# A hybrid decoder layer's list schedule: small VectorE instructions and the shared SBUF port, and a choice that is left open while the port is taken

## The chip, the cores and the metric

The kernel runs on one core of a Trainium2 chip. The metric is the device time of one execution in microseconds, as the median of several runs. Five engines work beside each other: TensorE (PE) for matmuls, with its weight loads shown apart (PEld), VectorE (DVE), ScalarE (ACT), GpSimd (POOL), and SyncE (SP), which issues the DMAs. "Busy" is the time in which an engine executes; "idle before" is the gap ahead of an instruction and the instruction or transfer that ended it.

## The reference, cut to what matters

One decoder layer, batch 1, 512 tokens, 1024 channels, all float32. Two attention branches run over the same normalized input, are merged by gates and followed by an MLP with 4096 hidden channels:

```python
h = rmsnorm(x, ln_mix_g[l])
proj = h @ w_in[l]
(dq, dk, dv, nq, kc, vc, ksl, vsl, kwn, vwn, ng, mg) = jnp.split(proj, split_at, axis=-1)
dq = rope(rmsnorm(dq.reshape(B, S, DIFF_HEADS, 2, HEAD_DIM), diff_q_norm_g[l]), pos)
...
y_diff = diff_attention(dq, dk, dv, lam, lambda_init, diff_subln_g[l])
...
y_nsa = nsa_attention(nq, k_cmp, v_cmp, k_slc, vsl.reshape(B, S, G, HEAD_DIM), k_win,
                      vwn.reshape(B, S, G, HEAD_DIM), nsa_gates)
merge = jax.nn.sigmoid(mg).reshape(B, S, 2, D)
mixed = merge[:, :, 0] * (y_diff @ w_proj_diff[l]) + merge[:, :, 1] * (y_nsa @ w_proj_nsa[l])
x = x + mixed @ w_out[l]
h = rmsnorm(x, ln_mlp_g[l])
x = x + jnp.square(jax.nn.relu(h @ w_mlp_up[l])) @ w_mlp_down[l]
```

The first branch is a differential attention of 8 heads (two softmaxes, one subtracted from the other with a factor lam); the second has 16 heads in 4 groups with a compressed, a selected and a windowed part.

## The kernel before, in words

**Precision.** Every float32 matmul is made of three with rounded operands. An operand is split into a high part (a cast) and a low part (what is left: operand minus high part), and the products high by high, low by high and high by low are summed. For weights the DMA brings `wraw` (128 x 1024), `whi` is its cast and `wlo` the subtraction, each done in two halves of 512 columns; both have two buffers, and so has `wraw`. The same splitting makes `qa` and `qb` from transposed queries, `kp` from transposed keys (one buffer; DMAs carry it on to `kk`), `ah` and `al` from transposed probabilities, `vt`, `big`, `kk` and others.

**Stages.** Up to some 665 us the kernel projects the input piece by piece (matmuls into `gb`), normalizes and rotates queries and keys (`str` are their inverse norms, made by POOL with a power, `t1r` and `t2r` the products of the rotation, `rw` the result), transposes them (`ptp`), and runs the score, softmax and value steps of both branches (`sb`, `p`, `sm`, `pta`, `av` for the first; `sbc`, `sc`, `st`, `smn`, `ptn`, `avn` for the second). A small side work makes the compressed keys (`hb`, `o`, `st2`, `ct1`, `ct2`). From some 665 us the branches' outputs are multiplied with their projections (`big`, `tm`, `kk`), then with w_out, and from some 700 us the MLP runs: matmuls of 512 columns without a break, for which weights are split.

**What sets the order.** The program does not issue instructions as it meets them. Each is recorded by `note` with a priority (the order of recording, with 15 places' advance for hot streams), what it depends on, the engines that may do it (`ways`) with a planned duration for each (`price`), and whether it uses the SBUF port that DVE and POOL share (`ported`). `flush` then plans the whole program, and issues all instructions in the order of planned starts, so that every engine's order is fixed before the kernel runs; line 357 is the one line that issues, and all rows of the trace carry it. The planner takes the engine that can go on first, and of its ready instructions the one with the best priority. `self.port` is the time until which the shared port is planned to be taken.

Some instructions may go to either of two engines: the cast `whi` to ACT or DVE, the subtraction `wlo` to DVE or POOL, the products `t1r` and `t2r` and their sum to DVE or POOL, some additions of `tm` to DVE or POOL, copies and other casts to ACT or DVE. Whichever engine the planner serves first, with that instruction on top, gets it.

Before the change, `ported` said no for any instruction whose largest operand has fewer than 64 elements a partition. An instruction that uses the port, met while the port was taken, was passed over if the engine had a ready one that doesn't use it; if it had none, the one with the best priority was tied to this engine, with its start put off until the port comes free.

Of the kernel before, what the change touches and what calls it, by code (L numbers as in the profile page):

```python
# [14 lines left out]
OP = mybir.AluOpType  # L15
# [116 lines left out]
class Sched:  # L132
# [34 lines left out]
    def price(self, eng, method, aps, k):  # L167
        if "accum_out" in k:
            aps = [x for x in aps if x is not k["accum_out"]]
        n = max(self.size(x) for x in aps)  # L170
        psum = any(self.tiles[x.tensor.name].space == "PSUM" for x in aps if x.tensor.name in self.tiles)
        if eng == "PE":
            if method == "transpose":
                return 113.0
            return max(113.0, 5.5 + self.size(aps[-1]) * 0.4315)
        if eng == "ACT":
            return (51 if psum else 93) + n * 0.8333 + (93 if "accum_out" in k else 0) + (
                93 if any(self.size(x) == 1 for x in aps[1:]) and n > 1 else 0)
        if eng == "DVE":
            ptr = sum(1 for x in aps[1:] if self.size(x) == 1) if n > 1 else 0  # L180
            if method in ("tensor_scalar", "tensor_copy") and not psum:
                return 69 + n * 0.52 + 61 * ptr
            if method == "memset":
                return 8 + n * 1.04
            if method == "reciprocal":
                return 69 + n * 6.25
            return 69 + n * 1.042 + 61 * ptr
        if eng == "POOL":
            if k.get("op") == OP.pow:
                return 300 + n * 165.0  # L190
            return 150 + n * 2.1
        return 20.0
# [2 lines left out]

    def ported(self, eng, method, aps, k):

        if max(self.size(x) for x in aps) < 64:
            return False
        if eng == "POOL":  # L200
            return k.get("op") != OP.pow
        return eng == "DVE" and method in self.TWICE and not any(
            self.tiles[x.tensor.name].space == "PSUM" for x in aps if x.tensor.name in self.tiles)

# [67 lines left out]
    def flush(self):  # L272
# [34 lines left out]
        while len(done) < len(ops):  # L307
            best = None
            for e in self.free:
                for h, k in ((self.wait[e], 2), (ok[e], 1)):  # L310
                    while h and h[0][k].left == -1:
                        heapq.heappop(h)
                t = self.free[e] if ok[e] else max(self.free[e], self.wait[e][0][0]) if self.wait[e] else None
                if t is not None and (best is None or t < best[0]):
                    best = (t, e)
            assert best is not None, "no instruction can go on"
            t, e = best
            while self.wait[e] and self.wait[e][0][0] <= t:
                _, p, op = heapq.heappop(self.wait[e])
                if op.left == 0:  # L320
                    heapq.heappush(ok[e], (p, op))
            p, op = heapq.heappop(ok[e])
            if op.port[e] and self.port > t:
                put_off = [(p, op)]
                while ok[e] and put_off[-1][1].port[e]:
                    z = heapq.heappop(ok[e])
                    if z[1].left == 0:
                        put_off.append(z)
                if not put_off[-1][1].port[e]:
                    p, op = put_off.pop()  # L330
                else:
                    p, op = put_off.pop(0)
                for z in put_off:
                    heapq.heappush(ok[e], z)
            op.eng = e
            op.start = max(t, self.port) if op.port[e] else t
            op.end = op.start + op.ways[e][1]
            if op.port[e]:
                self.port = op.end
            self.free[e] = op.end  # L340
            if op.dma:
                self.hw = max(op.end, self.hw) + op.dma[0]
                self.dma = max(self.hw + 650, self.dma) + op.dma[1]
                op.end = self.dma
            op.left = -1
            done.append(op)
            for u in op.users:
                u.ready = max(u.ready, op.end + self.lat(e, u.eng, u.deps[op]))
                self.arm(u)
            for b in op.bufs:  # L350
                b.left -= 1
                b.end = max(b.end, op.end)
                if b.left == 0 and b.group is not None:
                    self.held[b.group] -= 1
                    self.grant(b.group, b.end + 150)
# [71 lines left out]
def hybrid_block(ctx: ExitStack, tc: tile.TileContext, x, ln_mix_g, w_in, dqg, dkg, lq1, lk1, lq2, lk2,  # L427
# [137 lines left out]
    with ExitStack() as ps:  # L565
# [616 lines left out]
        def value_stream():  # L1182
# [87 lines left out]
            for p in range(2):  # L1270
                yield there(("pc", p))
                yield lambda p=p: ("n", p, NT - 1) in vtiles
                flush()
                vvar = cmp_values(p)
                for h in range(8):
# [373 lines left out]
```

## Time and profile before

| | us |
|---|---|
| median of 3 runs | 1097.47 |
| the three runs | 1095.7 to 1097.67 |
| the profiled execution's own time | 1096.69 |
| its span in the trace | 1094.9 |

The profiled execution has 1.8 us that lie outside the span. Times in the rows below are counted from the span's start. A row of a timeline gives the start, the duration (of several instructions in a row with gaps between them, the time from the first to the last), the engine, the operation, its output and inputs with buffer numbers left out, shapes, and the number of instructions; in brackets stands how long the engine was idle before, and for whom. A row by stretch gives the busy time of PE, PEld, DVE, ACT and POOL in it, then the granted clock of PE (1.00 is 2.4 GHz, 0.50 is 1.2 GHz), the share of the DMA engines and GB/s.

### The profile page before, as it was taken

What the parts mean: (1) busy time and instruction counts of PE and PEld (TensorE: products, weight loads), DVE (VectorE), ACT (ScalarE), POOL (GpSimd) and SP (SyncE); (2) the same over time, 40 slices, a digit from 0 to 9 for tenths busy, and PEclk for the clock granted to TensorE, in tenths of its full rate; (3) what the DMA queues carried; (4) which work ended last, traced back from release to release, by engine and by line L of the source; (5) the groups of instructions that cost most, each with busy time, mean ns of one, the idle gap of its engine ahead of it and who ended that gap; (6) DMA issues with size and microseconds to landing.
All of it is one profiled execution on the core that took longest, in us unless ns stands there. A gap on an engine that the chain in (4) does not pass through costs nothing.

```text
span 1094.9 us, 15737 instructions
## 1 busy us (share of the span) xinstructions
PE 1053.8 (96%) x5257; PEld 875.6 (80%) x5257; DVE 766.2 (70%) x1905; ACT 465.6 (43%) x1136; POOL 477.0 (44%) x475
## 2 busy tenths in 40 slices
PE   6999988899999999999999998999999999999998
PEld 5877867788787888887788886788888888888886
DVE  6779678899988999999989898556533323354232
ACT  4257335656464466665456563214222111242110
POOL 3745698348767372292212024423333222333221
PEclk9999988999999999999999999999999999999999
DMA  6362534642654224536363255622322223332232
GB/s 209 97 173 63 153 102 120 163 132 71 172 143 142 64 78 137 142 125 214 129 193 112 92 161 170 208 85 94 96 97 97 97 96 96 97 97 96 97 136 75
DMA packets 83616, 134.66 MB, mean 123 GB/s; under 512 B 8784, under 2 KB 33872, under 8 KB 83536
## 3 DMA queue, kind: packets, MB, share of 16 engines
q1 hardware_dynamic: 83536, 133.67, 39.7%
q8 instruction: 41, 0.67, 0.3%
q14 instruction: 39, 0.32, 0.1%
HBM read 106.64 MB, written 14.42 MB: 111 GB/s over the span
## 4 chain that ended last, share of the span: by engine, by line
PE 74%; DVE 12%; DMA 6%; POOL 4%; issue 2%; SPq 1%; ACT 1%; DVEq 0%; POOLq 0%; ACTq 0%
PE gb L357 38%; PE ga L357 22%; PE sb L357 4%; PE avn L357 4%; PE ptn L357 3%; DMA kk<-kp 3%; DVE p L357 2%; POOL str L357 1%; PE av L357 1%; POOL wlo L357 1%; SPq L357 1%; POOL t1r L357 1%; DVE al L357 1%; DVE sm L357 1%; DMA kk<-in_x_dram 1%
## 5 line engine op out<-in xcount | busy, mean ns | idle before, releaser
L357 POOL TENSOR_TENSOR wlo<-wraw,whi 128x512 fp32r<-128x512 f32 x203 | 289.0, 1432 | 522.7 <-ACT whi L357 396.2
L357 ACT CAST whi<-wraw 128x512 fp32r<-128x512 f32 (+2 forms) x217 | 130.0, 618 | 343.7 <-PE gb L357 167.0
L357 DVE CAST whi<-wraw 128x512 fp32r<-128x512 f32 x97 | 47.5, 489 | 199.7 <-PE ga L357 95.8
L357 PE MATMUL gb<-wlo,hTh 128*128 128x512 f32 (+2 forms) x352 | 136.0, 388 | 4.4 <-POOL wlo L357 2.4
L357 PE MATMUL gb<-whi,hTl 128*128 128x512 f32 (+2 forms) x352 | 135.0, 384 | 0.0
L357 PE MATMUL gb<-whi,hTh 128*128 128x512 f32 (+2 forms) x352 | 133.4, 388 | 1.5 <-ACT hTh L357 1.3
L357 DVE CUSTOM_DVE_ANT_0 p<-sb,cst 128x512 f32<-128x512 f32 (+2 forms) x192 | 92.1, 481 | 13.1 <-PE sb L357 11.7
L357 DVE TENSOR_TENSOR wlo<-wraw,whi 128x512 fp32r<-128x512 f32 (+1 forms) x111 | 92.2, 832 | 7.2 <-ACT whi L357 2.7
L357 ACT ACTIVATE p<-p,smn 128x512 f32<-128x512 f32 (+3 forms) x128 | 72.0, 563 | 26.6 <-DVE smn L357 26.2
L357 PEld LDWEIGHTS gb<-wlo,hTh 128*128 128x128 f32 x352 | 67.7, 192 | 14.8 <-POOL wlo L357 3.4
L357 PEld LDWEIGHTS gb<-whi,hTh 128*128 128x128 f32 x352 | 66.7, 191 | 11.5 <-ACT hTh L357 1.7
L357 PEld LDWEIGHTS gb<-whi,hTl 128*128 128x128 f32 x352 | 67.6, 192 | 10.3 <-DVE hTl L357 0.3
L357 DVE TENSOR_SCALAR p<-p,smn,gates 128x512 f32<-128x512 f32 (+3 forms) x128 | 66.9, 527 | 1.0
L357 PE MATMUL gb<-big,whi 128*128 128x512 f32 x192 | 65.1, 403 | 0.0
L357 PE MATMUL gb<-hTl,whi 128*128 128x512 f32 x160 | 64.7, 404 | 0.0
L357 PE MATMUL gb<-hTh,wlo 128*128 128x512 f32 x160 | 64.5, 403 | 0.0
L357 PE MATMUL gb<-hTh,whi 128*128 128x512 f32 x160 | 64.0, 400 | 0.0
L357 DVE TENSOR_TENSOR al<-ptn,ah 128x128 fp32r<-128x128 f32 (+3 forms) x128 | 61.3, 482 | 3.6 <-ACT ah L357 2.0
L357 PE MATMUL ga<-h2l,whi 128*128 128x512 f32 x160 | 62.5, 391 | 0.0
L357 PE MATMUL ga<-h2h,whi 128*128 128x512 f32 x160 | 62.4, 391 | 0.0
L357 PE MATMUL ga<-h2h,wlo 128*128 128x512 f32 x160 | 62.3, 390 | 0.0
L357 ACT CAST ah<-ptn 128x384 fp32r<-128x384 f32 (+3 forms) x98 | 41.2, 424 | 49.1 <-PE ptn L357 38.1
(248 smaller groups left out, 2634.7 us busy)
## 6 DMA issues: line engine op xcount, KB each, us to landing
wraw<-in_w_in_dram SPq DMA_DIRECT2D x36, 512.0 KB, 3.6
wraw<-in_w_mlp_up_dram SPq DMA_DIRECT2D x32, 512.0 KB, 3.8
wraw<-in_w_mlp_down_dram SPq DMA_DIRECT2D x32, 512.0 KB, 3.5
kk<-kp SPq DMA_DIRECT2D x48, 256.0 KB, 4.5
wraw<-in_w_in_dram SPq DMA_DIRECT2D x36, 256.0 KB, 3.2
big<-yd SPq DMA_DIRECT2D x16, 512.0 KB, 3.4
yd<-yo SPq DMA_DIRECT2D x8, 512.0 KB, 3.3
wraw<-in_w_proj_diff_dram SPq DMA_DIRECT2D x8, 512.0 KB, 4.3
```

What stands on the lines that cost most here:

```text
L357: op.ways[op.eng][0](*op.a, **op.k)
```

## The change

Three edits in the planner; no instruction's arithmetic changes, and PE and SP issue as many instructions as before.

1. `price`: a scalar_tensor_tensor of DVE on one element is planned 61 ns longer.
2. `ported`: the exemption of instructions with fewer than 64 elements holds for POOL alone. A small tensor_tensor, tensor_scalar, scalar_tensor_tensor or tensor_copy of DVE that has no operand in PSUM is now planned to wait for the port and to take it.
3. `flush`: where an engine has only ready instructions that need the port, and the port is taken, none is chosen. They stay ready, for either engine, and the engine is looked at again when the port comes free or when its next instruction gets ready, whichever is first.

```diff
         if eng == "DVE":
-            ptr = sum(1 for x in aps[1:] if self.size(x) == 1) if n > 1 else 0
+            ptr = sum(1 for x in aps[1:] if self.size(x) == 1) if n > 1 else method == "scalar_tensor_tensor"
...
     def ported(self, eng, method, aps, k):
 
-        if max(self.size(x) for x in aps) < 64:
-            return False
         if eng == "POOL":
-            return k.get("op") != OP.pow
+            return k.get("op") != OP.pow and max(self.size(x) for x in aps) >= 64
         return eng == "DVE" and method in self.TWICE and not any(
...
-                if not put_off[-1][1].port[e]:
+                go = not put_off[-1][1].port[e]
+                if go:
                     p, op = put_off.pop()
-                else:
-                    p, op = put_off.pop(0)
                 for z in put_off:
                     heapq.heappush(ok[e], z)
+                if not go:
+                    self.free[e] = min(self.port, self.wait[e][0][0]) if self.wait[e] else self.port
+                    continue
             op.eng = e
-            op.start = max(t, self.port) if op.port[e] else t
+            op.start = t
```

The numbers behind the names in the following rows are the program's own for its tiles. In all, DVE issues 2062 instructions in place of 1907, and POOL 342 in place of 480.

The first place is where the compressed keys are normalized and the rotated keys transposed (150 to 158 us in the trace). DVE before, from the last sum of a rotation on:

```order
L357 TENSOR_TENSOR t1r_419<-t1r_419,t2r_421 128x512
L357 TENSOR_SCALAR o_423<-o_423,st2_424 128x64
L357 TENSOR_TENSOR rw_391<-t1r_419,str_418 128x512
L357 TENSOR_TENSOR ct2_426<-o_423,ropes_172 128x32 x2
L357 TENSOR_TENSOR ct1_425<-o_423,ropec_171 128x64
L357 TENSOR_REDUCE str_460<-sqr_462 128x8
L357 CAST kp_431<-ptp_430 128x512
L357 TENSOR_TENSOR o_423<-ct1_425,ct2_426 128x64 x2
L357 TENSOR_TENSOR kp_431<-ptp_430,kp_431 128x512
```

DVE now:

```order
L357 TENSOR_TENSOR t1r_419<-t1r_419,t2r_421 128x512
L357 TENSOR_SCALAR o_423<-o_423,st2_424 128x64
L357 TENSOR_TENSOR rw_391<-t1r_419,str_418 128x512
L357 TENSOR_TENSOR ct1_425<-o_423,ropec_171 128x64
L357 TENSOR_TENSOR ct2_426<-o_423,ropes_172 128x32 x2
L357 CAST whi_436<-wraw_413 128x512
L357 TENSOR_TENSOR o_423<-ct1_425,ct2_426 128x64 x2
L357 TENSOR_TENSOR wlo_437<-wraw_413,whi_436 128x512
L357 CAST qa_434<-ptp_433 64x512
L357 TENSOR_TENSOR kp_431<-ptp_430,kp_431 128x512
```

DVE has got one cast of whi, one half of a wlo and the cast of qa, and has lost the cast of kp to ACT and a sum of squares to a later place.

POOL at the same place, before:

```order
L357 TENSOR_TENSOR str_418<-str_418,epsc_131 128x8
L357 TENSOR_TENSOR t2r_421<-rw_391,ropes_168 128x4x32
L357 TENSOR_TENSOR str_418<-str_418,mhalf_130 128x8
L357 TENSOR_TENSOR st2_424<-st2_424,epsc_131 128x1
L357 TENSOR_TENSOR wlo_428<-wraw_402,whi_427 128x512
L357 TENSOR_TENSOR st2_424<-st2_424,mhalf_130 128x1
L357 TENSOR_TENSOR wlo_437<-wraw_413,whi_436 128x512 x2
```

POOL now:

```order
L357 TENSOR_TENSOR str_418<-str_418,epsc_131 128x8
L357 TENSOR_TENSOR st2_424<-st2_424,epsc_131 128x1
L357 TENSOR_TENSOR str_418<-str_418,mhalf_130 128x8
L357 TENSOR_TENSOR st2_424<-st2_424,mhalf_130 128x1
L357 TENSOR_TENSOR wlo_437<-wraw_413,whi_436 128x512
```

POOL has one half of wlo_437 behind the power of st2 in place of two, and none ahead of it.

The second place is where the branches' outputs are projected (665 to 673 us in the trace). DVE before, from the first merge step on:

```order
L357 SCALAR_TENSOR_TENSOR tm_2051<-tm_2051,gb_1978 128x512
L357 SCALAR_TENSOR_TENSOR tm_2054<-tm_2054,gb_1979 128x512
L357 CAST whi_2047<-wraw_2036 128x512
L357 TENSOR_TENSOR tm_2055<-tm_2055,tm_2054 128x512
L357 SCALAR_TENSOR_TENSOR kk_2053<-tm_2052,kk_2053 128x512
L357 SCALAR_TENSOR_TENSOR kk_2053<-tm_2055,kk_2053 128x512
L357 SCALAR_TENSOR_TENSOR tm_2056<-tm_2056,gb_1980 128x512
L357 TENSOR_TENSOR big_1027<-yr_2058,big_1027 128x512
```

DVE now:

```order
L357 SCALAR_TENSOR_TENSOR tm_2051<-tm_2051,gb_1978 128x512
L357 TENSOR_TENSOR big_1027<-yr_2050,big_1027 128x512
L357 TENSOR_TENSOR tm_2052<-tm_2052,tm_2051 128x512
L357 CAST whi_2047<-wraw_2036 128x512
L357 SCALAR_TENSOR_TENSOR tm_2054<-tm_2054,gb_1979 128x512
L357 TENSOR_TENSOR wlo_2048<-wraw_2036,whi_2047 128x512
L357 SCALAR_TENSOR_TENSOR kk_2053<-tm_2052,kk_2053 128x512
L357 TENSOR_TENSOR tm_2055<-tm_2055,tm_2054 128x512
L357 SCALAR_TENSOR_TENSOR tm_2056<-tm_2056,gb_1980 128x512
L357 TENSOR_TENSOR big_1027<-yr_2058,big_1027 128x512
```

The sum tm_2052 and one half of wlo_2048, which POOL had, stand among DVE's rows, one kk has gone behind, and a big that came ahead of tm_2051 now follows it.

## Rows read from the trace of the kernel before

**Rows 1.** The page, its line of busy times, shares and instruction counts.

```profile
PE 1053.8 (96%) x5257; PEld 875.6 (80%) x5257; DVE 766.2 (70%) x1905; ACT 465.6 (43%) x1136; POOL 477.0 (44%) x475
```

**Rows 2.** Stages: PE, PEld, DVE, ACT, POOL busy, clock, DMA share, GB/s.

```profile
0.00:150.00 150.00, 138.47 (x687) 114.59 (x688) 113.58 (x271) 71.34 (x168) 86.75 (x97) 1.00 0.44 130
150.00:210.00 60.00, 50.13 (x249) 40.65 (x247) 49.20 (x120) 31.49 (x78) 39.30 (x46) 0.86 0.57 149
210.00:450.00 240.00, 232.10 (x1311) 196.90 (x1310) 221.44 (x631) 140.07 (x390) 139.91 (x184) 1.00 0.42 120
450.00:650.00 200.00, 197.22 (x1086) 164.88 (x1085) 186.74 (x567) 120.13 (x319) 66.81 (x57) 1.00 0.46 147
...
700.00:1094.90 394.90, 389.68 (x1732) 321.82 (x1731) 154.82 (x263) 84.03 (x148) 123.67 (x80) 1.00 0.31 102
```

**Rows 3.** Waits of PE: releaser, us in total, times, longest.

```profile
PE sb L357 <- DVE sm L357: 7.5, 10, 2.4
```

**Rows 4.** Stretches between changes of PE's clock, columns as in rows 2.

```profile
157.93:164.76 6.83, 6.08 (x17) 4.51 (x16) 5.00 (x9) 3.27 (x6) 4.41 (x8) 0.50 0.86 200
...
205.72:673.34 467.62, 453.19 (x2519) 381.06 (x2518) 431.97 (x1243) 272.86 (x739) 217.18 (x250) 1.00 0.44 131
673.34:676.76 3.42, 3.42 (x8) 2.75 (x9) 2.45 (x3) 0.69 (x2) 1.08 (x2) 0.51 1.01 374
```

**Rows 5.** Tiles wlo and sm by instruction: ns minimum, median, maximum, starts, forms.

```profile
L357 POOL TENSOR_TENSOR wlo<-wraw,whi x203: 389/1332/1763, 14.9 to 1080.9; 128x512 fp32r<-128x512 f32 x101, 128x400 fp32r<-128x400 f32 x1
...
L357 DVE TENSOR_TENSOR wlo<-wraw,whi x111: 568/693/1782, 9.2 to 1080.7; 128x512 fp32r<-128x512 f32 x110, 128x400 fp32r<-128x400 f32 x1
...
L357 DVE SCALAR_TENSOR_TENSOR sm<-sm,lam x32: 204/211/1234, 75.0 to 328.5; 128x1 f32<-128x1 f32 x32
L357 DVE TENSOR_SCALAR sm<-sm x32: 118/144/151, 75.1 to 328.8; 128x1 f32<-128x1 f32 x32
```

**Rows 6.** Groups of DVE by form: busy us, mean ns, idle before.

```profile
L357 DVE CAST whi<-wraw 128x512 fp32r<-128x512 f32 x97 | 47.5, 489 | 199.7 <-PE ga L357 95.8 <-PE gb L357 85.1 <-issue 12.8
...
L357 DVE TENSOR_TENSOR t2r<-rw,ropes 128x128 f32<-128x128 f32 x36 | 12.6, 367 | 0.0
```

**Rows 7.** Timeline at 28 us, then from 149.9 to 157.5 us.

```profile
28.14 0.50 PE L357 MATMUL gb<-wlo,hTh 128*128 128x512 f32 x1 [0.76 <-POOL wlo L357]
...
149.96 2.52 POOL L357 TENSOR_TENSOR wlo<-wraw,whi 128x512 fp32r<-128x512 f32 x2
150.02 1.27 DVE L357 TENSOR_SCALAR o<-o,st 128x64 f32<-128x64 f32 x1 [1.84 <-POOL st L357]
...
151.21 1.82 DVE L357 TENSOR_TENSOR rw<-t1r,str 128x512 f32<-128x512 f32 x1
...
157.46 0.70 PE L357 MATMUL ptp<-cst,rw 128*128 128x128 f32 x4 [2.76 <-DVE kp L357]
```

**Rows 8.** Timeline from 173 to 176 us.

```profile
173.21 1.76 POOL L357 TENSOR_TENSOR wlo<-wraw,whi 128x512 fp32r<-128x512 f32 x1
...
173.77 1.22 DVE L357 SCALAR_TENSOR_TENSOR sm<-sm,lam 128x1 f32<-128x1 f32 x1
...
175.65 0.80 PE L357 MATMUL gb<-wlo,hTh 128*128 128x512 f32 x1 [1.82 <-DVE wlo L357]
```

**Rows 9.** Timeline from 270.9 to 272.3 us.

```profile
270.96 1.26 POOL L357 TENSOR_TENSOR wlo<-wraw,whi 128x512 fp32r<-128x512 f32 x1
...
272.27 0.39 PE L357 MATMUL gb<-wlo,hTh 128*128 128x256 f32 x1 [1.68 <-POOL wlo L357]
```

**Rows 10.** Timeline from 665 to 674 us.

```profile
665.73 1.29 DVE L357 SCALAR_TENSOR_TENSOR tm<-tm,gb 128x512 f32<-128x512 f32 x2 [0.82 <-PE gb L357]
...
667.75 3.15 POOL L357 TENSOR_TENSOR wlo<-wraw,whi 128x512 fp32r<-128x512 f32 x2
...
672.58 2.36 DVE L357 TENSOR_TENSOR big<-yr,big 128x512 fp32r<-128x512 f32 x2
...
673.31 0.80 PE L357 MATMUL ga<-big,whi 128*128 128x512 f32 x1 [3.29 <-DVE big L357]
```

## The prediction, made before the changed kernel ran

> **What bounds the kernel now.** I read the busy shares first, then the stages, then what PE waits for, then the places. TensorE (PE) is busy 1053.8 of 1094.9 us, VectorE (DVE) 766.2, GpSimd (POOL) 477.0 [rows 1]. So PE bounds the kernel, and all that a schedule can win is PE's idle time, 41.1 us, and what a lowered clock costs. The stages say where that lies [rows 2]: 11.53 us in the first 150 (150.00 less 138.47), 9.87 in the next 60, 7.90 in 210 to 450, 2.78 in 450 to 650, and 5.22 in the MLP from 700 on; the rest is in 650 to 700. The same rows show DVE: 221.44 of 240 us and 186.74 of 200 in the two middle stages, hence nearly full there, but only 154.82 of 394.90 in the MLP. The reader should keep both facts: in the middle DVE is nearly full and yet PE hardly waits, since it has weight matmuls to put in between.
>
> Of PE's waits the largest sum goes to DVE's softmax sums (sm), 7.5 us in ten waits [rows 3]. Beside idle time there is the clock: PE ran at half of it (1.2 in place of 2.4 GHz) in some stretches; of two, 6.83 and 3.42 us long [rows 4], half is lost, 3.4 and 1.7 us. The longer one begins just after PE had stood for 2.76 us [rows 7], the shorter after 3.29 [rows 10]; the 1.68 us at 272 [rows 9] lie in a stretch of 467.62 us at the full clock [rows 4].
>
> **The change part by part.** Edit 1 adds 61 ns to the planned duration of DVE's 1-element scalar_tensor_tensor. The trace has 211 ns as median of 32 [rows 5]; the edit moves plans by 32 x 0.06 = 2 us of DVE in all and costs the chip nothing by itself: 0.
>
> Edit 2 makes DVE's small SBUF instructions wait for the port in the plan. Two forms of one element speak differently. The scalar_tensor_tensor on sm takes 204 at the least and 1234 ns at the most; the long one stands at 173.77 with 1.22 us, beside a POOL wlo of 1.76 us from 173.21 [rows 5, 8]. So it does wait for POOL. The TENSOR_SCALAR on sm is 118 to 151 ns in all 32 cases [rows 5], though the plan of before put it down whenever DVE was free: it never waits. For that form the edit postpones what need not be postponed. By the Trainium skill ("SBUF — State Buffer", Who interferes with whom) a DVE instruction with two SBUF inputs contends with a GpSimd instruction that reads SBUF, and one input outside the two-port modes does not; the trace agrees for the first form, which has two, and for the second, if one element is outside those modes, which no run here shows. By that rule the second form is put off for nothing, and if that lay on PE's path each time, the forecast would be 4.5 us later, at 1097.5.
>
> I count edit 2 at 0, with 32 x 0.14 = 4.5 us of needless delay as its bad end: one put off by mistake is only 0.14 us long and its engine does something else meanwhile.
>
> Edit 3 is the large one. When the port is taken and an engine has only instructions that need it, before tied the engine to the most urgent one; now the choice is made when the port comes free, or when something new is ready. Since the choice is left open, the other engine often takes it. The orders show it: of the wlo halves before tm_2051 (665.73 us [rows 10]), DVE gets 37 that POOL had, and in the MLP 62 more. Beside these, DVE gets 12 casts of whi that ACT had, 21 of the rope's t2r, 13 of its t1r and 4 tm additions before or about tm_2051.
>
> What that costs DVE. A wlo half is 0.693 us on DVE and 1.332 on POOL (medians) [rows 5]; a whi cast 0.49 and a t2r 0.37 (means, stretched ones in them) [rows 6]; t1r I take at 1.5 times a t2r, 0.55, and tm at 0.7 like a wlo. 37 x 0.693 + 12 x 0.49 + 21 x 0.37 + 13 x 0.55 + 4 x 0.7 = 25.6 + 5.9 + 7.8 + 7.2 + 2.8 = 49 us. By the orders a third of it, 16 us, lies before 200 us, where DVE idles for 36.4 of the first 150 us and 10.8 of the next 60 [rows 2]. The other 33 us fall into the middle, where it idles for 18.6 and 13.3 us [rows 2]. Against that, POOL loses 37 x 1.33 = 49 us of wlo alone, and each POOL wlo that is gone no longer holds up a DVE instruction or waits behind one; that return is between 0 and 49 us and no row prices it. In the MLP 62 x 0.69 = 43 us come on top of 154.82 in 394.90 us: DVE would be half busy, PE's matmuls go on, so 0.
>
> What PE gains, place by place.
>
> At 28 us PE waits 0.76 us for a POOL wlo [rows 7]. After has both halves on DVE in one row ahead of U and lam: 0 to -0.76, I take -0.5.
>
> At 150 to 158 us: DVE's o<-o,st takes 1.27 us and rw 1.82 beside a POOL pair of wlo (2.52 us from 149.96), and kp comes so late that PE stands for 2.76 us [rows 7]. In after POOL has one half of that pair, right behind the same pow, the other is DVE's and stands behind rw. So POOL holds the port for half as long, and rw ends some 1.26 us sooner (151.8 in place of 153.03). Behind rw, the transposes that it feeds, qa and kp follow sooner too; but a whi cast, a wlo half and a qa cast now stand ahead of kp's subtract, 0.49 + 0.69 + 0.67 = 1.85 us. From rw's end at 151.8, with 0.7 for ct and o and 0.68 for kp itself, they end at 155.0, where PE went on at 157.46 before: -2.4, if none of them waits for the transposes. Bounds: -2.4 and 0 (they wait so long that kp comes as before). I allow 0.7 for such waits and take -1.7. With 1.06 us left to wait I count the half-clock stretch that followed as gone, -3.4, since 1.68 us at 272 brought none. Together -5.1; if the idleness only moves, 0.
>
> At 173 to 176: PE waits 1.82 us for a DVE wlo behind the stretched sm [rows 8]. In after both halves of that wlo are on DVE; the POOL half that held sm up by a microsecond is gone, but it costs DVE 0.69, and the pta cast ahead of it now goes to DVE too. Gain and loss are alike: 0, between -5.2 (the 1.82 and, as at 157, 3.4 of clock) and +2 (as much again).
>
> At 272 PE waits 1.68 us for a wlo half that POOL begins only at 270.96, and for 1.26 us [rows 9]. In after both halves are on DVE, with a t2r between: 0.69 + 0.37 + 0.69 = 1.75 us for the pair, in a row of other rope work. 0 to -1.2; I take -0.3.
>
> At 668 to 673 DVE's tm, kk and the first big (its pair 2.36) run beside POOL's two wlo (3.15) and a tm, and PE waits 3.29 us for big [rows 10]. In after one of the wlo halves and that first POOL tm are DVE's. DVE's rows from tm_2051 to the first big_2058, at unstretched durations: nine of about 0.68 and a cast of 0.49, 6.6 us, so 665.73 + 6.6 = 672.3 in place of about 673.3: -1.0. With 2.3 us left I let the half-clock stretch stand (-1.7 if it goes).
>
> Sum of the gains: -0.5 - 5.1 - 0.3 - 1.0 = -6.9.
>
> New waits. All of PE's order in the attention part is new too, and DVE has 33 us more in the stages where it was nearly full. Bounds: 0, since there PE idled for only 10.7 us beside a DVE 92 and 93% busy [rows 2], and +16, half of the 33. I take +3, nearer to the first: what PE waits for there is hidden by weight matmuls, and POOL's load on the port falls.
>
> 1096.69 - 6.9 + 3 = 1092.8 for a profiled execution; the median of the runs, 1097.47, lies 0.8 above that one, so 1093.6, say 1093.
>
> **The rivals.** All of it comes good: the 173 place gives 5.2, the 668 place its 1.7, no new waits: 1097.5 - 6.9 - 6.9 = 1083.7. For it speaks that POOL has about a third fewer wlo before the MLP; against it the rows that now stand ahead of the same wlo.
>
> Nothing in sum: the places win, but idleness of the same size opens at others, with a half-clock stretch of its own (3.4 us): -6.9 + 3 + 3.4 leaves 1097.0, within 0.2%. For it: PE's order is new over 650 us, and which wait gets long is chance. That the change doesn't do what it says belongs here: the small instructions' stretch is a few us in all, and one of their forms has none [rows 5], so edit 2 may well be without effect; edit 3 moves work in any case.
>
> Slower: DVE becomes the bound in the middle. The 33 us do not fit into 31.9 us of DVE idleness, most of which are waits for inputs. If half of the 33 are not absorbed and POOL gives nothing back, PE waits some 16 us more: 1097.5 - 6.9 + 16 = 1106.6; with a third, 11, 1101.6. It decides from the point where unabsorbed work passes 7 us. For it: 92 and 93% busy [rows 2]. Against it: DVE's work and its stretch are in that busy time together, and POOL's wlo were part of the stretch. The Trainium skill ("Perfetto Trace Analysis", Optimizing Scalar/DVE Operations) says that moving work between GPSIMD and DVE might not help, as they share a read port; no run here shows yet which way that holds, and by that rule the result would be the rival of no sum.
>
> **How the numbers follow.** Forecast 1093 (1087 to 1095), chance 0.50; all good 0.08; nothing in sum 0.19; slower 0.23, at 1101 to 1107. About 0.2%, 2.2 us, is what a measurement of this kernel can tell from no change. So faster 0.58, same 0.19, slower 0.23. The range reaches from the good end, 1083, into the slower case, with a little over a third unabsorbed, 1103.
>
> **What would show it.** Right: no PE wait over 1 us at 157 and no half-clock stretch after it; sm's scalar_tensor_tensor without values over 1 us; POOL's busy time down by some 130 us (99 wlo at 1.33), DVE's up by less than the 92 counted (49 + 43); PE's idle time in 210 to 650 still near 11 us. Wrong: PE's waits for DVE in 210 to 650 at 20 us or more (then DVE bounds it); or the 157 place mended and a new half-clock stretch elsewhere (then nothing in sum); or DVE's 1-element TENSOR_SCALAR unchanged while its successors start later (edit 2 costs).

## The result, and the profile after

The changed kernel takes 1106.85 us (median of six runs, 1101.76 to 1108.54) against 1096.28 for the kernel before (six runs): a ratio of 1.0084, with an interval of 1.0068 to 1.0101. It is 10.6 us slower, where 4 us less were forecast. The profiled execution has a span of 1105.6 us, 10.7 more than before.

The page's line of busy times of the changed kernel, to be read against [rows 1]:

```profile
PE 1052.2 (95%) x5257; PEld 874.7 (79%) x5257; DVE 795.6 (72%) x2060; ACT 457.4 (41%) x1119; POOL 297.4 (27%) x337
```

The same stages as in [rows 2], of the changed kernel (PE, PEld, DVE, ACT, POOL busy, clock, DMA share, GB/s):

```profile
0.00:150.00 150.00, 136.78 (x677) 112.76 (x678) 115.36 (x297) 70.62 (x168) 57.30 (x71) 1.00 0.43 131
150.00:210.00 60.00, 47.31 (x247) 38.38 (x246) 46.54 (x125) 29.00 (x72) 29.30 (x34) 0.91 0.59 149
210.00:450.00 240.00, 225.47 (x1277) 192.03 (x1277) 216.43 (x663) 134.45 (x379) 118.99 (x159) 0.99 0.42 117
450.00:650.00 200.00, 194.79 (x1061) 161.91 (x1060) 184.44 (x568) 113.95 (x303) 54.69 (x45) 0.98 0.42 132
...
700.00:1105.60 405.60, 400.87 (x1782) 331.10 (x1780) 193.49 (x331) 88.10 (x155) 30.29 (x23) 1.00 0.32 104
```

PE is busy 1.6 us less than before and idle 53.4 us in place of 41.1: the whole loss is idleness. Stage by stage it grows by 1.7 us (0 to 150: 13.2 against 11.5), 2.8 (150 to 210: 12.7 against 9.9) and 9.1 (210 to 650: 14.53 + 5.21 = 19.7 against 10.7), and changes little after that. POOL has lost 180 us of work, DVE has gained only 29.4. In the middle DVE is not fuller than before: 216.43 us of 240, where it had 221.44.

The half-clock stretches of the changed kernel, columns as above, to be read against [rows 4]:

```profile
172.88:176.29 3.41, 3.05 (x14) 3.06 (x15) 2.19 (x8) 3.39 (x9) 0.74 (x2) 0.51 0.00 0
200.18:207.01 6.83, 5.13 (x19) 4.23 (x20) 5.23 (x16) 5.69 (x14) 1.29 (x1) 0.51 0.64 144
...
445.94:452.77 6.83, 5.16 (x15) 4.18 (x16) 4.66 (x13) 3.51 (x10) 1.29 (x1) 0.51 0.60 136
...
514.21:517.62 3.41, 3.41 (x9) 2.73 (x10) 2.93 (x6) 1.02 (x2) 1.90 (x2) 0.51 0.91 308
```

They sum to 20.5 us, and so do the four of the kernel before, two of them in [rows 4] and the other two here; only the places are others:

```profile
175.00:181.82 6.82, 6.17 (x21) 5.28 (x22) 6.22 (x14) 1.65 (x5) 6.74 (x6) 0.50 0.45 152
...
202.30:205.72 3.42, 3.17 (x14) 2.87 (x14) 2.44 (x12) 1.41 (x5) 0.10 (x1) 0.51 0.98 224
```

PE's largest waits in the changed kernel, but for one at the start that both kernels have (releaser, us in total, times, longest); the first had 7.5 us before [rows 3], the other two are new:

```profile
PE sb L357 <- DVE sm L357: 5.6, 4, 2.0
PE pta L357 <- DVE sm L357: 5.0, 1, 5.0
PE ptc L357 <- DVE kp L357: 3.9, 1, 3.9
```

One wait is 5.0 us long and one 3.9. In each a half-clock stretch of 6.83 us begins while PE still stands: at 200.18 in the wait from 196.66 to 201.63, and at 445.94 in the one from 443.67 to 447.61. PE is busy for 5.13 and 5.16 us of these two stretches. The timeline of the first wait, one row each of SP, ACT, DVE and PE:

```profile
189.18 3.43 SPq L357 DMA_DIRECT2D kk<-kp  x4
...
193.00 0.19 ACT L357 ACTIVATION_READ_ACCUMULATOR ysq<-yt,sm 128x1 f32 x1
...
200.26 0.59 ACT L357 CAST kp<-ptp 128x512 fp32r<-128x512 f32 x1 [7.08 <-DMA kk<-kp]
...
200.88 0.69 DVE L357 TENSOR_TENSOR kp<-ptp,kp 128x512 fp32r<-128x512 f32 x1 [5.00 <-ACT kp L357]
...
201.63 0.69 PE L357 MATMUL pta<-cst,p 128*128 128x128 f32 x2 [4.97 <-DVE sm L357]
```

The tile kp has one buffer. Four copies carry it into kk; only when the last has landed may the next cast write it. Here the copies are issued from 189.18 on, and ACT, whose next instruction is that cast, stands for 7.08 us. DVE's next instruction is kp's subtraction, so DVE stands too, for 5.00 us, with the softmax sums behind it, and PE waits for these. The name in PE's row, sm, is only the last link. The second place, on four engines:

```profile
437.60 3.46 SPq L357 DMA_DIRECT2D kk<-kp  x4
...
443.04 0.62 PE L357 MATMUL sb<-kk,qa 128*128 128x512 f32 x2
...
446.25 0.59 ACT L357 CAST kp<-ptp 128x512 fp32r<-128x512 f32 x1 [4.74 <-DMA kk<-kp]
...
446.87 0.69 DVE L357 TENSOR_TENSOR kp<-ptp,kp 128x512 fp32r<-128x512 f32 x1 [4.14 <-ACT kp L357]
...
447.61 1.12 PE L357 MATMUL ptc<-cst,pc 128*128 128x128 f32 x4 [3.94 <-DVE kp L357]
```

The kernel before has the same copies and the same single buffer. What its tile kp answers (idle time before its instructions, times, and the copies' landing):

```profile
  DMA kk<-kp: 11.4, 6
...
DMA to landing us min/median/max: 2.9/4.5/6.5
```

and what that of the changed kernel answers:

```profile
  DMA kk<-kp: 20.4, 5
...
DMA to landing us min/median/max: 2.9/4.9/9.4
```

Before, engines stand 11.4 us for these copies. PE's longest wait behind them is 2.40 us, in the trace of the kernel before:

```profile
198.62 0.69 DVE L357 CAST kp<-ptp 128x512 fp32r<-128x512 f32 x1 [2.84 <-DMA kk<-kp]
...
199.84 0.50 PE L357 MATMUL sb<-kk,qa 128*128 128x256 f32 x2 [2.40 <-DVE sm L357]
```

After, it is 20.4 us, and both long waits stop ACT, DVE and PE at once. A third place is not in these 20.4 us, since its row names no releaser ("issue"):

```profile
288.85 0.59 ACT L357 CAST kp<-ptp 128x512 fp32r<-128x512 f32 x1 [4.42 <-issue]
...
289.76 0.50 PE L357 MATMUL gb<-whi,hTh 128*128 128x512 f32 x1 [1.80 <-ACT rw L357]
```

The same tile's answer counts it with the copies from the other side: ACT's casts into kp wait 16.2 us for them, three times, which is 7.08 + 4.74 + 4.42. With it engines stand 24.8 us.

### The profile page after: what moved, and what is told of

Its sections match the earlier page's. It is cut to its first block, busy times and chain, and to the rows that moved or that the text cites. A ratio compares the mean times of both kernels' runs of the same rounds, so it can differ in the third digit from the quotient of the medians.

```text
span 1105.6 us, 15611 instructions
## 1 busy us (share of the span) xinstructions
PE 1052.2 (95%) x5257; PEld 874.7 (79%) x5257; DVE 795.6 (72%) x2060; ACT 457.4 (41%) x1119; POOL 297.4 (27%) x337
## 4 chain that ended last, share of the span: by engine, by line
PE 69%; DVE 13%; DMA 6%; POOL 5%; issue 2%; ACT 2%; SPq 2%; DVEq 0%; ACTq 0%; POOLq 0%
PE gb L357 35%; PE ga L357 21%; PE sb L357 4%; DMA kk<-kp 3%; PE avn L357 3%; DVE p L357 3%; PE ptn L357 3%; POOL str L357 2%; SPq L357 2%; DVE rw L357 1%; DVE wlo L357 1%; POOL sm L357 1%; PE av L357 1%; PE hb L357 1%; DVE t1r L357 1%
## 5 line engine op out<-in xcount | busy, mean ns | idle before, releaser
L357 POOL TENSOR_TENSOR wlo<-wraw,whi 128x512 fp32r<-128x512 f32 x102 | 137.1, 1353 | 610.6 <-DVE whi L357 396.0
L357 ACT CAST whi<-wraw 128x512 fp32r<-128x512 f32 (+1 forms) x204 | 122.3, 617 | 348.8 <-PE gb L357 183.9
L357 DVE TENSOR_TENSOR wlo<-wraw,whi 128x512 fp32r<-128x512 f32 (+1 forms) x212 | 147.2, 722 | 6.0 <-ACT whi L357 1.4
L357 DVE CUSTOM_DVE_ANT_0 p<-sb,cst 128x512 f32<-128x512 f32 (+2 forms) x192 | 91.7, 481 | 11.7 <-PE sb L357 10.6
L357 PEld LDWEIGHTS gb<-whi,hTl 128*128 128x128 f32 x352 | 67.1, 191 | 10.2 <-DVE hTl L357 0.8
L357 PE MATMUL gb<-big,whi 128*128 128x512 f32 x192 | 68.8, 414 | 1.4 <-DMA big<-yd 1.4
L357 ACT CAST ah<-ptn 128x256 fp32r<-128x256 f32 (+3 forms) x99 | 41.7, 422 | 60.2 <-PE ptn L357 52.4
L357 DVE TENSOR_SCALAR p<-p,smn,gates 128x512 f32<-128x512 f32 (+3 forms) x128 | 64.0, 508 | 1.2
```

The lines of the kernel that those rows point to most:

```text
L357: op.ways[op.eng][0](*op.a, **op.k)
```

## The experiments

**Is it the copies out of kp?** The theory: the loss comes from engines that stand in order behind a cast into kp (A). The rival: DVE has too much work, and kp only shows where (B). The exchange below leaves every engine's order as it is, but three of the four copies read a tile that is never rewritten, so that kp is free after the first copy; kk then does not hold all the keys, and the copies' number and sizes stay. It was made in both kernels.

```diff
-                    Q.dma_start(f(dst[s][d * 64:(d + 1) * 64]), f(kp[s * 64:(s + 1) * 64]))
+                    other = f(hTh[s * 64:(s + 1) * 64, 0].rearrange("p k n -> p (k n)")).rearrange("p (a n) -> p a n", a=2)
+                    real = s == 0 and d == 0
+                    sched.note([("SP", "dma_start", lambda o, i, real=real, other=other:
+                                 nc.sync.dma_start(o, i if real else other))],
+                               (f(dst[s][d * 64:(d + 1) * 64]), f(kp[s * 64:(s + 1) * 64])), {})
```

The changed kernel with it:

> The changed kernel, every engine's order as it is, but three of the four transfers that copy kp into kk read another tile that is never rewritten, so kp's only buffer is free after the first of the four (the keys in kk are wrong for that reason; sizes and counts of transfers are as before). Theory A (the loss sits in the two places where the whole machine stands behind a cast into kp that waits for the transfers out of it, 5.0 us at 196 and 3.9 at 443, each followed by 6.8 us at half clock, 3.4 lost): both waits shrink to under 2 us, 8 to 16 us gone, 1091 to 1099. Theory B (DVE has too much work, waits for kp only show where): these waits are replaced by others, 1103 or more.

Measured: 1086.4 us, ratio to the kernel before 0.9906 (0.9887 to 0.9925). The kernel before with it:

> The same exchange in the kernel before, its order as it is (keys in kk wrong likewise). Theory A: it has one such place, 2.4 us at 199 with 1.7 us of clock behind it, so 1091 to 1095, and the distance to the changed kernel with the same exchange is under 4 us. Theory B: 1093 to 1096, and the distance stays at 8 or more.

Measured: 1087.26 us, 0.9919 (0.9901 to 0.9937). So the exchange gives 20.5 us in the changed kernel and 9 in the one before, more than A had counted in both, and the distance between the two shrinks from 10.6 to -0.9 us, with every engine's order unchanged in either. B, which wanted 8 or more, falls. Two stages of the changed kernel with the exchange, columns as in the stages above:

```profile
150.00:210.00 60.00, 53.34 (x308) 44.02 (x307) 56.09 (x162) 37.07 (x100) 33.78 (x43) 1.00 0.63 162
210.00:650.00 440.00, 426.22 (x2374) 358.11 (x2373) 406.42 (x1233) 249.32 (x679) 172.65 (x198) 1.00 0.42 129
```

and of the kernel before with it:

```profile
150.00:210.00 60.00, 52.17 (x278) 42.78 (x277) 54.07 (x144) 35.41 (x92) 41.25 (x50) 0.91 0.59 157
210.00:650.00 440.00, 430.17 (x2404) 362.87 (x2404) 409.65 (x1192) 260.64 (x707) 205.23 (x238) 1.00 0.43 133
```

The clock column is 1.00 now where the changed kernel had 0.91 and 0.99. But the two do not come to the same in the same way: the changed one is idle 13.8 us in 210 to 650 (440 less 426.22) against 9.8, and has no half-clock stretch, while the other has 17.1 us of them, of which at most half, 8.5, is lost.

**Are two places enough?** The same exchange at two of the twelve fillings of kp, those whose copies PE waits for at 196 and 443:

```diff
-                    real = s == 0 and d == 0
+                    real = s == 0 and d == 0 or len(calls) not in (5, 11)
```

> The changed kernel in its order, with kp freed early at only two of its twelve fillings, those whose copies PE waits for at 196 and at 443 (three of the four copies there read another tile, so the keys in kk are wrong at these two). With all twelve freed it was 20.5 us faster. If the two places carry the loss, 5.0 + 3.9 us of waiting and 3.4 + 3.4 of clock go, 1106.85 - 15.7 = 1091, between 1088 and 1095. If the loss is spread over the fillings, 1098 or more.

Measured: 1095.77 us (1091.89 to 1100.68), 0.9983 (0.9963 to 1.0002). PE's two waits shrink from 4.97 and 3.94 to 0.40 and 0.49 us. The two places carry 11 of the 20.5 us: by profile 7.8 us of PE's idleness (45.6 in place of 53.4) and 2.6 of its busy time. The rest hangs on the other ten; the wait at the third place is still there (1.71 us), and with all twelve freed it is gone. The forecast for two places had counted 15.7 us, some 5 too much: the time at half clock fell by 10.3 us, PE's busy time not by half of that.

**Which edit brings it?** The third edit alone (the choice left open, the rest as before):

> The third edit alone (choice left open) on the kernel before. It moves nearly all the low halves that the whole change moves (208 on DVE in place of 111). Theory B: 1103 or more, as the changed kernel. Theory A: the time depends on where the casts into kp fall, 1090 to 1110, and PE's waits of over 2 us are behind kp.

Measured: 1101.1 us, 1.0042 (1.0025 to 1.0058). The first and second alone:

> The first and second edits alone (61 ns more, small instructions of DVE wait for the port) on the kernel before; 107 low halves on DVE, about as before. Theory B: within 3 us of 1096.5, since DVE's work doesn't change. Theory A: 1090 to 1110 by where the casts into kp fall.

Measured: 1096.0 us, 0.9994 (0.998 to 1.0007): no change. The first and third:

> The first and third edits (61 ns more for 32 instructions, choice left open), small instructions exempt as before. If the third edit brings the loss by a rule of its own, 1099 to 1108 like the third alone (1101). If the place of the casts into kp is luck of the plan, the 61 ns may move it either way: 1090 to 1108, and the time follows PE's waits behind kp.

Measured: 1105.36 us, 1.0091 (1.0076 to 1.0106). The second and third:

> The second and third edits, without the 61 ns. By a rule of its own: 1099 to 1108. By luck: 1090 to 1108, following PE's waits behind kp.

Measured: 1105.41 us, 1.0082 (1.006 to 1.0104). All four kernels with the third edit are slower, by 4.5 to 10.6 us; the one without it is not. The third alone brings about half of what the whole brings, and with either of the others it brings all of it, though the first and second alone bring nothing. In each of the four PE waits about as long near 443 us. In the third alone a DVE row stands there, then PE's:

```profile
441.05 0.69 DVE L359 CAST kp<-ptp 128x512 fp32r<-128x512 f32 x1 [5.09 <-DMA kk<-kp]
...
442.45 0.55 PE L359 MATMUL ptc<-cst,pc 128*128 128x128 f32 x3 [4.21 <-DVE al L359]
```

In the first and third ACT's row stands there, then PE's, and in the second and third, where ACT's cast stands 6.00 us, PE's row reads as the last line:

```profile
443.09 0.58 ACT L359 CAST kp<-ptp 128x512 fp32r<-128x512 f32 x1 [5.10 <-DMA kk<-kp]
...
444.46 0.47 PE L359 MATMUL ptn<-cst,p 128*128 128x128 f32 x1 [3.86 <-DVE kp L359]
```

```profile
448.37 0.47 PE L357 MATMUL ptn<-cst,p 128*128 128x128 f32 x1 [4.75 <-DVE kp L357]
```

So this wait is in all four plans with the third edit. Without that edit it is absent in the kernel before, and in the first and second alone it is there in a smaller form: the cast stands 1.75 us and PE 1.17. Over all fillings engines stand 13.0 to 24.8 us behind the copies in the four, and 10.7 and 11.4 in the two.

**Does it go when the planner knows the copies?** The planner's expectation of a copy within the chip was 0.625 us to issue, 0.65 until it starts, and 0.73 to carry (256 KB at 360 bytes a ns): by its formula 0.625 + 0.65 + 4 x 0.73 = 4.2 us for four. In the trace kp is held for 11.1 us at 189 (to 200.26) and 8.65 at 437 (to 446.25). The edit changes this expectation, which only the copies out of kp have, to 0.78 + 0.65 + 4 x 1.5 = 7.4 us by the same formula (6.8 in the text below, which leaves the 0.65 out), and nothing else, so the plan puts other instructions ahead of the next cast into kp:

```diff
+            if inside:
+                op.dma = (780.0, 1500.0)
```

The changed kernel with it:

> The changed kernel, whole, but the planner expects more of the copies out of kp: 0.78 us to issue each and 1.5 us to carry it, 6.8 us for the four, about what the trace has, in place of some 3.7. So it plans the next cast into kp later and puts other instructions ahead. Theory A (the loss is the planner's ignorance of this transfer): PE's waits behind kp fall from 15 us with the clock to under 6, 1088 to 1098. Rival: the wait goes on costing since the data are needed at that time, and only its place changes: 1102 or more.

Measured: 1087.58 us, 0.9933 (0.9917 to 0.9949). What its tile kp answers, idle time behind the copies:

```profile
  DMA kk<-kp: 3.4, 2
```

The kernel before with it:

> The same expectation of the copies in the kernel before. Theory A: its waits for kp (5.7 us on DVE and 5.7 on ACT, of which PE sees 2.4 and 1.7 of clock) fall too: 1090 to 1096, and the distance to the changed kernel with the same edit is under 4 us. Rival: 1094 to 1099, distance 6 or more.

Measured: 1088.68 us, 0.9935 (0.9918 to 0.9951); engines stand 0.3 us behind the copies, once. Both come out faster than both kernels, 1.1 us apart. In this pair A stands: with the copies longer in the plan, the difference between the two is gone. The third edit alone with this expectation:

> The third edit alone with the longer expectation of the copies (0.78 us to issue, 1.5 to carry). If that expectation takes away what the third edit brings in loss, whatever else is changed: 1085 to 1091. If it was luck with the whole change: 1094 or more.

Measured: 1094.15 us (1091.26 to 1095.23), 0.9974 (0.9963 to 0.9985). That is 7 us off the third edit alone, and just inside the second expectation (1094 or more), not the first. The kernel before gained as much by the same expectation, so the third edit alone still costs what it did: 0.9974 against 0.9935 is 4.3 us, where 1.0042 was 4.6. Engines stand only 2.0 us behind the copies there. For the third edit alone, then, the waits for the copies are not shown to be what it costs.

A still longer expectation (0.9 us and 2.0 us in place of 0.78 and 1.5, 9.6 us for four by the formula), in the changed kernel:

> The changed kernel with a still longer expectation of the copies (0.9 us to issue each, 2.0 to carry; 8.9 us for the four, near the longest in the trace, 9.4). DVE still waited 3.4 us for them at the shorter one. If waiting is what counts, 1084 to 1088; if casts into kp now come too late for the scores that need kk, 1089 to 1095.

Measured: 1090.12 us, 0.9935 (0.992 to 0.9951), in the second expectation. In the kernel before:

> The kernel before with the same still longer expectation. It waited only 0.3 us for the copies at the shorter one, so nothing to win there: 1087 to 1092.

Measured: 1082.06 us (1081.23 to 1083.25), 0.9866 (0.9851 to 0.9881), better than expected and the fastest version of all: the kernel before with these two numbers in its planner, 14 us under it. In neither does an engine stand behind the copies any more, and yet the changed one is 8.1 us behind. The middle of the changed one:

```profile
210.00:650.00 440.00, 423.43 (x2356) 355.06 (x2355) 409.79 (x1227) 244.11 (x665) 179.43 (x202) 1.00 0.42 127
```

and of the other:

```profile
210.00:650.00 440.00, 435.22 (x2435) 368.92 (x2435) 409.97 (x1210) 266.25 (x719) 207.77 (x239) 1.00 0.44 135
```

PE is idle 16.6 us there against 4.8, and DVE's busy time is the same to 0.2 us.

**Is that DVE's load?** Before the merge the changed kernel with this expectation has 78 of 166 wlo halves on DVE, the other 46. Here the second halves are tied to POOL, which gives 46:

```diff
-                self.split(hi[:, c], lo[:, c], self.raw[k][:, c], lo_engs=self.todo[k][1])
+                self.split(hi[:, c], lo[:, c], self.raw[k][:, c],
+                           lo_engs=("POOL",) if c.start and "POOL" in self.todo[k][1] else self.todo[k][1])
```

> The changed kernel with the still longer expectation of the copies (0.9 and 2.0 us), and the second half of every wlo tied to POOL where POOL may do it, so that DVE has 46 of the 166 halves before the merge, as in the kernel before with that expectation, in place of 78. If DVE's load is what costs 8 us there: 1080 to 1086. If it is the left-open choice itself: 1088 or more, PE's waits for sm as large as with 78 (8 us).

Measured: 1096.91 us (1093.97 to 1099.51), 1.001 (0.9999 to 1.0021). The middle:

```profile
210.00:650.00 440.00, 422.68 (x2342) 355.00 (x2341) 402.96 (x1208) 248.19 (x680) 187.60 (x215) 0.99 0.42 128
```

PE is idle 17.3 us there with 46 halves on DVE, and 16.6 with 78, so fewer halves on DVE do not bring it down. It is one plan, and PE's waits moved in it: those for sm fell from 8.0 to 3.9 us, where the expectation had them stay, and others took their place. The first and second edits with that expectation, also 46 halves:

> The first and second edits alone with the still longer expectation; 46 halves on DVE too. If the third edit (by DVE's load or by itself) is what costs: 1080 to 1085. If small instructions that wait for the port in the plan cost: 1087 or more.

Measured: 1088.49 us, 0.9936 (0.9921 to 0.9951), against 0.9866 without these edits and 0.9935 with the third on top of them. That is in the second expectation: in this plan the first and second edits cost nearly all of the distance, some 7 us, and the third adds nothing clear, though the idleness in the middle is 7.6 us without it and 16.6 with it. A third expectation (1.0 and 2.5 us, 11.7 for four by the formula), in the changed kernel:

> The changed kernel with a third expectation of the copies (1.0 and 2.5 us, 10.4 us for four, over the longest in the trace); 79 halves on DVE before the merge. If the change costs by DVE's load: at least 4 us more than the kernel before with the same expectation; 1087 to 1093. If the 8 us were luck: within 3 us of it.

Measured: 1095.05 us, 0.9992 (0.9982 to 1.0001). In the kernel before:

> The kernel before with that third expectation; 41 halves on DVE before the merge. No wait for the copies is left to win: 1080 to 1088.

Measured: 1099.52 us (1095.89 to 1102.09), 1.0024 (1.0003 to 1.0045), far over what was expected. Here the changed one is the faster, by 4.5 us, which neither expectation had. So from pair to pair the distance is -0.9, -1.1, +8.1 and -4.5 us: with the waits for the copies gone, no sign is left that would hold. The kernel before alone ranges from 1082.06 to 1099.52 us with these expectations of one transfer.

One thing holds through all of them. PE's idle time in 210 to 650 us, and the time at half clock up to the last matmuls, by profile:

| choice while the port is taken | kernel | median us | idle 210 to 650 | half clock |
|---|---|---|---|---|
| tied (as before) | before | 1096.28 | 10.7 | 20.5 |
| tied | b_kpfree | 1087.26 | 9.8 | 17.1 |
| tied | b_kpprice | 1088.68 | 8.4 | 17.1 |
| tied | b_kpprice2 | 1082.06 | 4.8 | 10.2 |
| tied | b_kpprice3 | 1099.52 | 11.1 | 20.5 |
| tied | e12_only | 1096.0 | 9.9 | 13.7 |
| tied | e12_kpprice2 | 1088.49 | 7.6 | 13.7 |
| open | after | 1106.85 | 19.7 | 20.5 |
| open | e3_only | 1101.1 | 18.3 | 10.2 |
| open | e13 | 1105.36 | 19.0 | 20.5 |
| open | e23 | 1105.41 | 20.4 | 20.5 |
| open | a_kpfree | 1086.4 | 13.8 | 0 |
| open | a_kpfree2 | 1095.77 | 16.6 | 10.2 |
| open | a_kpprice | 1087.58 | 16.2 | 3.4 |
| open | a_kpprice2 | 1090.12 | 16.6 | 0 |
| open | a_kpprice3 | 1095.05 | 16.7 | 6.8 |
| open | a_kpprice2_pool | 1096.91 | 17.3 | 10.2 |
| open | e3_kpprice | 1094.15 | 18.2 | 3.4 |

Every kernel with the open choice has more idleness in the middle (13.8 us or more) than any with the tied one (11.1 or less). The kernels of the second group whose waits for the copies were shortened or taken away have less half clock than most of the first (0 to 10.2 us against 10.2 to 20.5). Where all twelve fillings were treated, the mean of the second group has some 8 us more idleness and some 12 us less half clock than that of the first, of which at most half is lost, so that the two largely offset each other. That the rest of the whole change's loss is the waits for the copies, the exchange shows; for the third edit alone it is not shown.

## Why the prediction was wrong, point by point

The forecast was 1093 us, with one range of 1087 to 1095 and, further on, a wider one of 1083 to 1103; 1106.85 lies outside both. The gains that it sought came; the step that failed is the term for new waits.

**Where PE would gain: right, nearly to the size.** At 28 us the wait is gone. At 150 to 158 the changed kernel's rows, to be read against [rows 7], are:

```profile
149.24 0.24 DVE L357 TENSOR_SCALAR o<-o,st 128x64 f32<-128x64 f32 x1
149.40 0.68 DVE L357 TENSOR_TENSOR rw<-t1r,str 128x512 f32<-128x512 f32 x1
...
150.83 1.96 POOL L357 TENSOR_TENSOR wlo<-wraw,whi 128x512 fp32r<-128x512 f32 x1 [2.50 <-DVE whi L357]
...
152.97 0.63 PE L357 MATMUL ptp<-cst,rw 128*128 128x128 f32 x4 [0.18 <-DVE kp L357]
```

No POOL instruction lies beside o and rw, they take 0.24 and 0.68 us in place of 1.27 and 1.82, and PE waits 0.18 us in place of 2.76, without a half-clock stretch behind it: the 5.1 us of the sum are there, with 0.9 more of idleness. At 173 the wlo wait is 1.02 us in place of 1.82 [rows 8], but a new one, of 2.42 us for a whi cast, comes ahead of it:

```profile
173.24 0.58 PE L357 MATMUL hb<-U,whi 128*128 128x260 f32 x1 [2.42 <-ACT whi L357]
...
177.78 0.50 PE L357 MATMUL gb<-wlo,hTh 128*128 128x512 f32 x1 [1.02 <-DVE wlo L357]
```

That is 1.6 us more of waiting, against a half-clock stretch of 3.41 us where one of 6.82 was, at most 1.7 us less; "gain and loss are alike" holds. At 272 the wait for wlo is gone, and the 1.80 us behind the third place of kp stand some 17 us further on. At 668 two waits for big stand where one was [rows 10]:

```profile
684.26 0.50 PE L357 MATMUL ga<-big,whi 128*128 128x512 f32 x1 [1.14 <-DVE big L357]
...
691.90 0.50 PE L357 MATMUL ga<-big,whi 128*128 128x512 f32 x1 [1.90 <-DVE big L357]
```

Together they are 3.04 us, where the one was 3.29, but the half-clock stretch is gone: some 1.7 us, and 0.25 of waiting, in place of the 1.0 expected.

**The MLP: right.** 62 halves were moved and cost nothing; the chain's last pieces are 10.2 us later as a whole (1014.23 in place of 1004.00) and of the same length (43.52 us).

**Edits 1 and 2: right as far as they go.** Alone they change nothing (0.9994); with the 9.6 us expectation of the copies they are some 7 us slower, and whether that is their price or one plan's luck is not shown. The changed kernel's rows for sm (ns minimum, median, maximum), to be read against [rows 5]:

```profile
L357 DVE SCALAR_TENSOR_TENSOR sm<-sm,lam x32: 202/216/612, 74.0 to 329.0; 128x1 f32<-128x1 f32 x32
...
L357 DVE TENSOR_SCALAR sm<-sm x32: 115/145/150, 76.1 to 329.1; 128x1 f32<-128x1 f32 x32
```

The form with two SBUF inputs, which reached 1234 ns, reaches 612; the other, never stretched, is as before.

**DVE's bill: far too high.** 49 + 43 = 92 us were counted, 29.4 came, in 155 instructions more, while POOL's busy time fell by 180 in place of 130. The return, which the prediction put between 0 and 49 us and did not count, was by difference some 60 us over the whole kernel. By the Trainium skill ("SBUF — State Buffer", SBUF: two separate sides) the pair of ports that both engines share is an exclusive lock, and the loser blocks for the whole instruction. The rows agree: with half as many wlo on POOL, one of 512 columns takes 726 ns in the mean on DVE in place of 834, and 1353 on POOL in place of 1439, and o and rw above take 0.24 and 0.68 us where no POOL instruction lies beside them.

**New waits: the step that failed.** The prediction gave them +3 us, between 0 and +16. Measured, PE's idleness in 210 to 650 grew by 9.1 us, and in 150 to 210 by 2.8 although the place at 157 had won 2.6. With the gains as forecast (-6.9), a span that is 10.7 us longer leaves 17.6 us for new waits and their clock, more than the upper bound of 16. That bound was half of the 33 us by which DVE was to get fuller in the middle; DVE's busy time in 210 to 650 is 400.87 us, where it had 408.17. What was missing in the sum is a term for the copies out of kp. The rows of before show it: PE waits 2.4 us for sm at 199, its longest such wait [rows 3], and behind that sm stood a cast into kp that waited for a DMA. That wait had a place in the trace and no place in the sum, where new waits were sought in DVE's load alone. By what the exchange gives in each kernel, the term is 20.5 - 9.0 = +11.5 us for the copies, which leaves -0.9 for all the rest, where the prediction had -3.9. Of its signs of being wrong one came true: the place at 157 is mended, and half-clock stretches stand elsewhere, at 200 and 446; the prediction had expected no change in sum from that.

**The rival that DVE becomes the bound** gave 1101 to 1107, and the time lies there, but for another reason: DVE is less busy in 210 to 450 than before, and with 46 halves on DVE in place of 78 PE's idleness in the middle stays (17.3 us, one plan). The rule of the Trainium skill ("Perfetto Trace Analysis", Optimizing Scalar/DVE Operations) that moving work between the two engines might not help was cited with it; here the move did neither harm nor good that can be told from the plan's other effects (1087.58 against 1088.68, and 1095.05 against 1099.52, but 1090.12 against 1082.06). "Nothing in sum" is what is left when the copies are taken out of these two plans by the exchange.

**What stays open.** Why the left-open choice lengthens PE's idleness in the middle, by some 4 to 12 us from pair to pair, isn't settled; one plan speaks against DVE's share of the halves, and nothing else was tried. That an engine which is no longer tied to an instruction that needs the port takes the cast into kp as soon as the plan thinks its buffer free (it reads PSUM, and in the plan needs no port) would explain why that edit runs into the copies. It was only argued, and the third edit alone costs as much with the longer expectation as without. And differences of up to 8 us between two plans that no wait of ours explains show how much of any such change is the luck of one order.

## What to carry to other kernels

When a plan's rule is changed, look first for the waits that the plan does not know of: here a transfer whose planned length was too short cost 9 us in one order and 20.5 in another, and where an engine met it too early, everything behind it in that engine's order stood (7.08 us at 193). PE's row names the last link (a softmax sum); the first link is found by following the row before it on each engine that stood still. To judge a planner's rule, run it under several values of a neighbouring number: to the kernel before, two longer lengths of that transfer were worth 7.6 and 14.2 us and a third cost 3.2, and one pair alone would have said either thing of the rule.

## What the runs showed of the hardware that was not expected

The same 256 KB copy within the chip landed 2.9 us after its issue at the least and 9.4 at the most in the changed kernel, and 6.5 at the most before; the group at 189 us, next to loads of weights on the same queue, kept its buffer for 11.1 us (189.18 to 200.26). And taking 180 us of work off POOL and giving 155 more instructions to DVE lengthened DVE's busy time by only 29.4 us.
